# Expert layers of a two-block transformer: where the next expert's tokens are transposed, how weight rows lie on partitions, and when the two down sums run

## The chip, the cores and the metric

One core of one Trainium2 chip runs the whole program in one launch. The metric is the device time in microseconds (us) from launch to end; the kernel before took 3669.67 us as the median of three runs (3669.27 to 3676.42). The core has a matmul engine (PE; its weight loads, PEld, run beside the matmuls), VectorE (DVE), ScalarE (ACT), GpSimd (POOL), SyncE (SP, which here issues loads and stores) and 16 DMA engines.

## The reference

Two blocks over 1024 tokens of width 1024, all float32. The first block has two layers, each a mixer (differential attention, then pooling) with a layer norm, and behind it a mixture of experts with a layer norm. The second block (retention, latent attention, gated linear attention) isn't touched. The change lies in the experts, which run once in each of the two layers of the first block:

```python
# router: one of 4 groups per token, the best 2 of its 8 experts, gates from two softmaxes
xin = xf[tok_pad].reshape(NB, MOE_BLOCK, D)            # tokens sorted by expert, blocks of 128
def run_block(args):
    xb, e = args
    h = jax.nn.silu(xb @ w_gate[e]) * (xb @ w_up[e])   # [128, 1024] @ [1024, 512]
    return h @ w_down[e]                               # [128, 512] @ [512, 1024]
y = lax.map(run_block, (xin, blk_e)).reshape(P, D)
out = jnp.zeros((N, D)).at[tok_pad].add(y * w_pad[:, None])
```

There are 32 experts in a layer; each has 2 MB of gate, 2 MB of up and 2 MB of down weights. 1024 tokens with two experts each make 64 tokens per expert on the average; an expert works in one tile of 128.

## The kernel before, in words

**One expert.** `Moe.run` (L759) goes through the 32 experts of a layer. The tokens of an expert come by an indirect DMA on GpSimd (`gather`, L695) out of `hd` in DRAM into one of four buffers `xg`, one token per partition. `x_t` (L698) transposes them: eight 128 x 128 transposes on PE (L95) into two PSUM tiles `tp` of four blocks each, and a split of each tile (L80, L81) into a high part (ACT, `xgh`) and a low part (DVE, `xgl`), both float32r. In a transpose the tokens are the operand that PE loads, the identity the one that streams. A product in this kernel is three matmuls (`mm3`, L85 to L87): high x high, high x low, low x high.

`gate_up` (L705) takes four pieces of weights of 1 MB each, gate and up for the first 512 rows, then gate and up for the last 512 rows. Each piece is 4 x 3 = 12 matmuls of 512 columns into one of two PSUM sums `gu`; silu (ACT, L720) and a product (DVE, L721) make the hidden values `sgu`. `turn_mid` (L724) transposes these in four blocks (L732) into one tile `tp` and splits it into `hh` and `hl`. `down` (L736) takes two more pieces, the left 512 and the right 512 columns of the down weights, each 12 matmuls into a sum `accy`; ACT scales the sum by the gate (L750), DVE adds the residual from `xg` (L751), and GpSimd scatters the result `yo` to `yd` in DRAM (L752).

**Weights.** SP loads each piece (`load_raw`, L98) into one of nine buffers as they come by turns. Partition p of a piece takes row p of each block of 128 rows: 512 columns, 2 KB, in one run, four of them per partition. ACT and DVE split a piece (`split_w`, L106) into one of four buffers `wcut`, high part first.

**The order of an expert's steps.** The hidden values of expert e-1 are transposed in the middle of the gate and up products of expert e, and its down sums follow these. The text of the loop body at L774 to L785 is, in short:

```python
x = nxt
if e + 1 < 32:
    nxt = self.x_t(buf(e + 1), pool, ps)               # the next expert's tokens
between = lambda: mid.append(self.turn_mid(sg, pool, ps))
nsg = self.gate_up(None, None, x, pool, ps, None if e else nc.gpsimd, between if e else None)
if e > 0:
    down(e - 1, mid[0])
if e + 3 < 32:
    gather(e + 3)
```

The tiles `xgh`, `xgl`, `hh`, `hl`, `yo`, and in PSUM `gu` (two kinds), `accy` and `tp` have two buffers each; the eight PSUM banks are all taken. The token buffer that `gather(e + 3)` fills is the one that `down(e - 1)` has just read.

**What sets the order on the engines.** The text above isn't the order in which an engine works. When the program is built, a planner goes through all instructions with an estimate of the time of each. On every engine it takes the instruction that stands first in the text among those whose operands and buffers are there by its estimate, so an instruction further down may go ahead of one that has to wait in the plan. On the chip each engine then works through its own list strictly in order, and waits by semaphores. SP's list of loads is planned in the same way; a load waits until its buffer has been read.

A rare loop behind the experts (L792 to L810) takes the tokens beyond an expert's 128th with the same helpers and one buffer of weights (`OnePiece`); the trace has no round of it: 64 gathers are all.

Of the kernel before, what the change touches and what calls it, by code (L numbers as in the profile page):

```python
# [27 lines left out]
def host_consts():  # L28
# [12 lines left out]
    # a token's number and its row in the results, less 2048  # L41
# [15 lines left out]
    # rotary frequencies of the second block  # L57
# [12 lines left out]
class Ctx:  # L70
# [18 lines left out]
    def transpose_split(self, src, hi, lo, ps, scale=None):  # L89
        """src [128, 8, 128] f32 -> hi/lo [128, 8, 128-slice] f32r views, transposed by block."""  # L90
        nc = self.nc
        for g in range(2):
            tp = ps.tile([P, 4, P], F32, tag="tp", name=self.name("tp"))
            for k in range(4):
                nc.tensor.transpose(tp[:, k], src[:, 4 * g + k], self.ident)  # L95
            self.split(tp, hi[:, 4 * g:4 * g + 4], lo[:, 4 * g:4 * g + 4])

    def load_raw(self, view, pool, tag):  # L98
        """one piece of weights [128, 2048] as it comes; view: as its columns lie"""
        raw = pool.tile([P, 2048], F32, tag=tag, name=self.name("wraw"))  # L100
        a, b = view.shape[1:]
        raw = raw.rearrange("p (a b) -> p a b", b=b)
        self.nc.sync.dma_start(raw, view)
        return raw

    def split_w(self, raw, pool, tag, lo_eng=None, steps=1):  # L106
        """the same in two float32r parts"""
# [8 lines left out]
    def rsqrt(self, pool, v, shape):  # L116
        """1/sqrt(v) of a few columns"""
        y = pool.tile(shape, F32, tag="rs_y", name=self.name("rs_y"))
        self.nc.gpsimd.tensor_tensor(y, v, self.mhalf[:, 0:shape[1]], op=ALU.pow)  # L119
        return y  # L120


class Weights:
    """buffers of streamed weights: slots (pool, tag) that take the pieces as they come by turns, and one of the split ones"""
# [8 lines left out]
    def load(self, view, slot=None):  # L133
        if slot is None:
            slot = self.slots[self.turn % len(self.slots)]
            self.turn += 1
        return self.g.load_raw(view, *slot)
# [5 lines left out]
class OnePiece:  # L143
    """the same with one buffer of each kind, for loops"""
# [4 lines left out]
    def load(self, view):  # L149
        raw = self.raw.rearrange("p (a b) -> p a b", b=view.shape[2])  # L150
        self.g.nc.sync.dma_start(raw, view)
        return raw
# [7 lines left out]
def phase_qkv(g, x_in, v_sb, fill):  # L160
    """queries and keys of differential attention, transposed, turned and split, to DRAM; values to v_sb"""
# [3 lines left out]
    with tc.tile_pool(name="p1", bufs=1) as p1, tc.tile_pool(name="p1w", bufs=2) as pw, \  # L165
# [4 lines left out]
        for t in range(NT):  # L170
# [4 lines left out]
            g.transpose_split(xn, xh[:, :, t * P:(t + 1) * P], xl[:, :, t * P:(t + 1) * P], ps)  # L175
# [15 lines left out]
                # the halves of the tokens outermost: the first product needs only half of them  # L191
# [42 lines left out]
class Attention:  # L234
    """differential attention of layer 0 up to its normalised heads, transposed: oT"""
# [30 lines left out]
    def spare(self):  # L266
        """a buffer [128, 1024] of the first head's, before its load"""
# [4 lines left out]
    def load(self, h):  # L272
        """queries (both parts on the partitions) and keys (each part twice) of both maps of a head"""
# [14 lines left out]
    def scores(self, h, i):  # L288
        """p0 / s0 - lambda p1 / s1 up to the factor 1 / s0"""
# [66 lines left out]
    def norm(self, h):  # L356
        """rms norm of a head: (o / s0) / sqrt(mean((o / s0) ** 2) + eps)"""
# [22 lines left out]
    def norm_last(self, k):  # L380
        """the same for tiles k and 7 - k of the last head, with its transposes"""
# [32 lines left out]
            # tiles of queries in pairs of a long and a short row of scores; the steps of a pair overlap with those of its neighbours  # L414
# [38 lines left out]
def layer_norm(g, pool, z, dst, gb, eps=1e-5):  # L453
    """dst = (z - mean) / sqrt(var + eps) * gain + bias over the free axis of [128, 1024]"""
# [15 lines left out]
def norm_stats(g, pool, z, eps=1e-5):  # L470
    """scale and shift that normalise the rows of [128, 1024]"""
# [14 lines left out]
def norm_apply(g, z, stats, gb):  # L486
    """the layer norm in place, spread over three engines"""
# [14 lines left out]
class Moe:  # L502
    """mixture of experts of one layer"""

    def __init__(self, g, layer, wp, pool, h, hd, yd):
# [9 lines left out]
        # the pieces of the weights in the order of their use  # L515
        wg, wu, wd = (a[n][layer] for n in ("moe_w_gate", "moe_w_up", "moe_w_down"))
        rows = lambda w, kb: w[kb * 512:kb * 512 + 512].rearrange("(k p) c -> p k c", p=P)
        cols = lambda w, n: w[:, n * 512:n * 512 + 512].rearrange("(k p) c -> p k c", p=P)
        self.views, self.raws = [], []
        for e in range(33):  # L520
            if e < 32:
                self.views += [rows(w[e], kb) for kb in range(2) for w in (wg, wu)]
            if e > 0:
                self.views += [cols(wd[e - 1], n) for n in range(2)]

    def prefetch(self, n):
        # the last pieces leave the middle slots, then the first to the stage that follows
        for _ in range(n):
            left = len(self.views)
            self.raws.append(self.wp.load(self.views.pop(0), self.wp.slots[(6 if left > 3 else 9) - left] if left < 7 else None))  # L530
# [5 lines left out]

    def turn(self, t, ps, pool):
        """one tile of tokens, transposed"""
# [11 lines left out]
    def logits(self, t, hT, ps):  # L550
        """router logits of one tile of tokens"""
# [9 lines left out]
    def temp(self, pool, lead, T, trail, n, dt=F32):  # L561
        """[128, *lead, T, *trail], T up to 4, of one size for all T"""
# [6 lines left out]
    def onehot(self, pool, src, n, tab, tag):  # L569
        """maximum over the last axis and the one-hot of its first place"""  # L570
# [11 lines left out]
    def route(self, t0, t1, pool, ps):  # L582
        """experts, gates and places of the tokens of tiles t0 to t1 - 1; the tables of the first window of slots"""
# [27 lines left out]
        # places: the assignments of the tiles before, and of the tokens before in the same tile  # L611
# [11 lines left out]
        # gates  # L623
# [69 lines left out]
    # one expert  # L693
# [4 lines left out]
    def x_t(self, xg, pool, ps):  # L698
# [3 lines left out]
        g.transpose_split(xg.rearrange("p (k d) -> p k d", d=P), xh, xl, ps)  # L702
        return xh, xl

    def gate_up(self, wg, wu, x, pool, ps, lo_eng=None, between=None):  # L705
        g, nc = self.g, self.g.nc
        acc = [ps.tile([P, 512], F32, tag=f"acc{j}", name=g.name("gu")) for j in range(2)]
        for kb in range(2):
            if kb == 1 and between is not None:
                between()  # L710
            for j, w in enumerate((wg, wu)):
                if w is None:
                    wh, wl = self.next_w(lo_eng)
                else:
                    wh, wl = self.wp.split(self.wp.load(w[kb * 512:kb * 512 + 512].rearrange("(k p) c -> p k c", p=P)))
# [8 lines left out]
    def turn_mid(self, sg, pool, ps):  # L724
        """the hidden values, transposed"""
# [4 lines left out]
        sv = sg.rearrange("p (k d) -> p k d", d=P)  # L730
        for k in range(4):
            nc.tensor.transpose(tp[:, k], sv[:, k], g.ident)  # L732
# [3 lines left out]
    def down(self, wd, mid, xg, gate, yidx, pool, ps, no_dep):  # L736
        """gate[:, 0] * (mid @ wd) + gate[:, 1] * xg to the rows yidx"""
# [3 lines left out]
        for n in range(2):  # L741
            if wd is None:
                wh, wl = self.next_w()
            else:
                wh, wl = self.wp.split(self.wp.load(wd[:, n * 512:n * 512 + 512].rearrange("(k p) c -> p k c", p=P)))
            acc = ps.tile([P, 512], F32, tag="accy", name=g.name("accy"))
            for k in range(4):
# [1283 lines left out]
```

## Time and profile before

| | |
|---|---|
| three runs, median | 3669.67 us (3669.27, 3669.67, 3676.42) |
| span of the profiled execution, first to last instruction | 3678.1 us |
| time of that execution around its span | not listed |
| PE busy in the span | 3337.8 us (91%) |
| DVE / ACT / POOL busy | 2438.9 (66%) / 1825.4 (50%) / 802.7 us (22%) |
| mean granted clock of PE | 0.944 |
| experts of layer 0 | about 715 to 1335 us of the span |
| experts of layer 1 | about 1655 to 2275 us of the span |

Busy shares are averages over stages with different limits, so a stage is read by itself. Times within the trace count from the first instruction. A matmul's duration includes its way through the array, and the next one starts before it ends: the distance between two starts is what one costs (about 0.229 us for 512 columns), not its 0.39 us. L12 is line 12 of the kernel. `tp<-ident,xg` reads: tile `tp` written from `ident` and `xg`.

### The profile page before, as it was taken

How to read it: one execution, taken by the hardware profiler on the slowest of the kernel's cores; microseconds unless marked ns; L12 is line 12 of the kernel's file. 1: busy time of each engine (PE TensorE's matmuls, PEld its weight loads, DVE VectorE, ACT ScalarE, POOL GpSimd, SP SyncE). 2: the span in 40 equal slices, each digit the busy share in tenths (PEclk: the TensorE clock that was granted, in tenths of full speed). 3: DMA queues.
4: the chain of work that ended last, by engine and by line, in shares of the span. 5: the costliest groups of instructions: out<-in, count | busy, mean ns of one | idle time of the engine just before them, and what ended most of it. 6: DMA issues, size and time to landing. Idle time of an engine off the chain costs nothing.

```text
span 3678.1 us, 44264 instructions
## 1 busy us (share of the span) xinstructions
PE 3337.8 (91%) x16820; PEld 2742.3 (75%) x16820; DVE 2438.9 (66%) x2912; ACT 1825.4 (50%) x2509; POOL 802.7 (22%) x591
## 2 busy tenths in 40 slices
PE   8889899799998969979999986699989899998988
PEld 7777777688877758768887765586777688776876
DVE  5564887699988886568998877734256435324753
ACT  3123673388866643317887765212447411234761
POOL 0000441223311123022332211533002223300120
PEclk9999999799999989979999998799999999999999
DMA  6554533499998970238999997311222541123144
GB/s 224 186 205 144 146 81 128 166 369 378 372 363 312 324 250 24 94 138 307 377 371 372 336 318 262 106 36 23 78 103 80 173 133 36 29 72 98 67 132 157
DMA packets 404046, 695.79 MB, mean 189 GB/s; under 512 B 43898, under 2 KB 140956, under 8 KB 403764
## 3 DMA queue, kind: packets, MB, share of 16 engines
q1 hardware_dynamic: 383092, 650.91, 52.5%
q0 software_dynamic: 18432, 33.60, 2.5%
q10 hardware_dynamic: 2304, 8.39, 0.6%
q8 instruction: 135, 2.21, 0.3%
q14 instruction: 83, 0.68, 0.1%
HBM read 625.59 MB, written 98.66 MB: 197 GB/s over the span
## 4 chain that ended last, share of the span: by engine, by line
PE 34%; issue 14%; POOL 6%; DVE 5%; ACT 2%; DMA 2%; POOLq 0%; SPq 0%; ACTq 0%; DVEq 0%
PE A L85 4%; PE A L87 4%; PE A L86 4%; PE acc L87 3%; PE acc L85 3%; PE acc L86 3%; POOL xg L695 3%; PE o L1712 1%; PE T L1691 1%; DMA mx<-mixd 1%; PE S L1659 1%; PE o L1703 1%; POOL rs_y L119 1%; PE S L1660 1%; PE S L1661 1%
## 5 line engine op out<-in xcount | busy, mean ns | idle before, releaser
L81 DVE TENSOR_TENSOR wcut<-wraw,wcut 128x2048 fp32r<-128x2048 f32 (+1 forms) x393 | 878.4, 2263 | 48.6 <-ACT wcut L80 46.2
L80 ACT ACTIVATE wcut<-wraw 128x2048 fp32r<-128x2048 f32 (+1 forms) x401 | 753.1, 1896 | 64.6 <-PE gu L87 43.9
L86 PE MATMUL gu<-wcut,xgh 128*128 128x512 f32 x1024 | 404.9, 395 | 7.3 <-DVE wcut L81 7.3
L85 PE MATMUL gu<-wcut,xgh 128*128 128x512 f32 x1024 | 407.0, 402 | 0.0
L87 PE MATMUL gu<-wcut,xgl 128*128 128x512 f32 x1024 | 402.0, 393 | 0.0
L85 PE MATMUL A<-h,whi 128*128 128x512 f32 (+1 forms) x736 | 288.0, 392 | 6.2 <-ACT h L80 3.3
L87 PE MATMUL A<-h,wlo 128*128 128x512 f32 (+1 forms) x736 | 282.8, 384 | 3.8 <-DVE wlo L81 3.8
L86 PE MATMUL A<-h,whi 128*128 128x512 f32 (+1 forms) x736 | 283.4, 385 | 0.9 <-DVE h L81 0.9
L752 POOL DMA_INDIRECT yd<-yo,idx x64 | 75.7, 1182 | 915.4 <-DVE yo L751 898.2
L695 POOL DMA_INDIRECT xg<-hd,idx x64 | 229.6, 3588 | 44.8 <-DVE idx L685 24.1
L80 ACT ACTIVATE whi<-wraw 128x1024 fp32r<-128x1024 f32 (+2 forms) x86 | 71.1, 856 | 337.2 <-PE A L86 252.9
L86 PEld LDWEIGHTS gu<-wcut,xgh 128*128 128x128 f32 x1024 | 193.1, 189 | 49.8 <-DVE wcut L81 12.2
L87 PEld LDWEIGHTS gu<-wcut,xgl 128*128 128x128 f32 x1024 | 192.5, 188 | 41.0
L85 PEld LDWEIGHTS gu<-wcut,xgh 128*128 128x128 f32 x1024 | 191.8, 188 | 40.0 <-ACT wcut L80 1.6
L86 PE MATMUL accy<-wcut,hh 128*128 128x512 f32 x512 | 213.7, 417 | 0.1
L85 PE MATMUL accy<-wcut,hh 128*128 128x512 f32 x512 | 208.7, 408 | 0.0
L87 PE MATMUL accy<-wcut,hl 128*128 128x512 f32 x512 | 207.9, 406 | 0.2
L81 DVE TENSOR_TENSOR wlo<-wraw,whi 128x1024 fp32r<-128x1024 f32 (+2 forms) x86 | 82.5, 974 | 177.1 <-ACT whi L80 176.9
L85 PEld LDWEIGHTS A<-h,whi 128*128 128x128 f32 x736 | 145.6, 198 | 34.3 <-ACT h L80 4.4
L87 PEld LDWEIGHTS A<-h,wlo 128*128 128x128 f32 x736 | 144.8, 197 | 31.6 <-DVE wlo L81 4.7
L86 PEld LDWEIGHTS A<-h,whi 128*128 128x128 f32 x736 | 145.4, 198 | 27.6 <-issue 3.1
L750 ACT ACTIVATE yo<-accy,sg 128x512 f32<-128x512 f32 x128 | 88.2, 689 | 153.1 <-PE accy L87 152.6
(509 smaller groups left out, 7825.6 us busy)
## 6 DMA issues: line engine op xcount, KB each, us to landing
wraw<-in_moe_w_gate SPq DMA_DIRECT2D x128, 1024.0 KB
wraw<-in_moe_w_up SPq DMA_DIRECT2D x128, 1024.0 KB
wraw<-in_moe_w_down SPq DMA_DIRECT2D x128, 1024.0 KB
spare<-in_ada_w SPq DMA_DIRECT2D x48, 512.0 KB
wraw<-in_w_in SPq DMA_DIRECT2D x40, 512.0 KB
y<-yd SPq DMA_DIRECT2D x16, 1024.0 KB
wraw<-in_attn_w_qkv SPq DMA_DIRECT2D x12, 1024.0 KB
mx<-mixd SPq DMA_DIRECT2D x24, 512.0 KB
```

The lines of the kernel that those rows point to most:

```text
L80: self.nc.scalar.activation(hi, src, AF.Copy)
L81: (lo_eng or self.nc.vector).tensor_tensor(lo, src, hi.bitcast(F32), op=ALU.subtract)
L85: mm(out, wh, xh, start=start, stop=False)
L86: mm(out, wh, xl, start=False, stop=False)
L87: mm(out, wl, xh, start=False, stop=stop)
L119: self.nc.gpsimd.tensor_tensor(y, v, self.mhalf[:, 0:shape[1]], op=ALU.pow)
L695: self.g.nc.gpsimd.indirect_dma_start(out=xg, out_offset=None, in_=self.hd, in_offset=bass.IndirectOffsetOnAxis(ap=idx, axis=0), bounds_ch ...
L750: nc.scalar.activation(y[:, sl], acc, AF.Copy, scale=gate[:, 0])
L752: st = nc.gpsimd.indirect_dma_start(out=self.yd, out_offset=bass.IndirectOffsetOnAxis(ap=yidx, axis=0), in_=y, in_offset=None, bounds_chec ...
L1659: nc.tensor.matmul(s[:, c:c + w], qs[0:96, 0, q], ks[0:96, 0, c:c + w], start=True, stop=False)
L1660: nc.tensor.matmul(s[:, c:c + w], qs[0:96, 0, q], ks[0:96, 1, c:c + w], start=False, stop=False)
L1661: nc.tensor.matmul(s[:, c:c + w], qs[0:96, 1, q], ks[0:96, 0, c:c + w], start=False, stop=not last)
```

## The change

In words:

- **Next tokens.** `x_t(e + 1)` is called inside `gate_up(e)`, between its first and its second half, behind `turn_mid(e - 1)`, and no longer ahead of `gate_up(e)`. For expert 0 there is no `turn_mid` and `x_t(1)` is called alone there.
- **Weight rows in pairs.** Partition p of a block of 256 rows takes rows 2p and 2p + 1. A gate or up piece has still 512 rows, now two runs of 4 KB per partition; a down piece is now 256 full rows of 1024 columns, one run of 8 KB per partition. To match, the transposes of the tokens and of the hidden values read every second column of a block of 256 (`pair_blocks`).
- **Down sums.** A down piece now serves both halves of the columns for half of the rows. Both sums are open over both pieces: piece 0 gives 6 matmuls to each sum, piece 1 the other 6, and then both sums are scaled and added.

The diff, without comments, and without the same edits in the helper classes that pass a width `b` along:

```diff
-    def transpose_split(self, src, hi, lo, ps, scale=None):
+    def transpose_split(self, src, hi, lo, ps):
...
-                nc.tensor.transpose(tp[:, k], src[:, 4 * g + k], self.ident)
+                nc.tensor.transpose(tp[:, k], src[4 * g + k], self.ident)
...
-        raw = raw.rearrange("p (a b) -> p a b", b=b)
-        self.nc.sync.dma_start(raw, view)
-        return raw
+    def load_into(self, raw, view, b=None):
+        by = lambda n: raw.rearrange("p (a b) -> p a b", b=n)
+        self.nc.sync.dma_start(by(view.shape[2]), view)
+        return by(b or view.shape[2])
...
+def even_blocks(x):
+    return [x[:, k] for k in range(KD)]
+def pair_blocks(x):
+    v = x.rearrange("p (a q j) -> p a j q", q=P, j=2)
+    return [v[:, k // 2, k % 2] for k in range(x.shape[1] // P)]
...
+    def rows(w, kb):
+        return w[kb * 512:kb * 512 + 512].rearrange("(a p j) c -> p a (j c)", p=P, j=2), 512
+    def down_rows(w, kb):
+        return w[kb * 256:kb * 256 + 256].rearrange("(a p j) c -> p a (j c)", p=P, j=2), D
...
-        rows = lambda w, kb: w[kb * 512:kb * 512 + 512].rearrange("(k p) c -> p k c", p=P)
-        cols = lambda w, n: w[:, n * 512:n * 512 + 512].rearrange("(k p) c -> p k c", p=P)
...
-                self.views += [rows(w[e], kb) for kb in range(2) for w in (wg, wu)]
+                self.views += [self.rows(w[e], kb) for kb in range(2) for w in (wg, wu)]
...
-                self.views += [cols(wd[e - 1], n) for n in range(2)]
+                self.views += [self.down_rows(wd[e - 1], kb) for kb in range(2)]
...
-        g.transpose_split(xg.rearrange("p (k d) -> p k d", d=P), xh, xl, ps)
+        g.transpose_split(pair_blocks(xg), xh, xl, ps)
...
-        for k in range(4):
-            nc.tensor.transpose(tp[:, k], sv[:, k], g.ident)
+        for k, b in enumerate(pair_blocks(sg)):
+            nc.tensor.transpose(tp[:, k], b, g.ident)
...
-        for n in range(2):
-            if wd is None:
-                wh, wl = self.next_w()
...
-            acc = ps.tile([P, 512], F32, tag="accy", name=g.name("accy"))
-            for k in range(4):
-                g.mm3(acc, hh[:, k], hl[:, k], wh[:, k], wl[:, k], k == 0, k == 3)
-            sl = slice(n * 512, n * 512 + 512)
+        cols = [slice(n * 512, n * 512 + 512) for n in range(2)]
+        accs = [ps.tile([P, 512], F32, tag="accy", name=g.name("accy"), bufs=2) for _ in cols]
+        for kb in range(2):
+            wh, wl = self.next_w() if wd is None else self.one_w(self.down_rows(wd, kb))
+            for acc, sl in zip(accs, cols):
+                for j in range(2):
+                    k = 2 * kb + j
+                    g.mm3(acc, hh[:, k], hl[:, k], wh[:, j, sl], wl[:, j, sl], k == 0, k == 3)
+        for acc, sl in zip(accs, cols):
             nc.scalar.activation(y[:, sl], acc, AF.Copy, scale=gate[:, 0])
             nc.vector.scalar_tensor_tensor(y[:, sl], xg[:, sl], gate[:, 1], y[:, sl], op0=ALU.mult, op1=ALU.add)
...
-                x = nxt
-                if e + 1 < 32:
-                    nxt = self.x_t(buf(e + 1), pool, ps)
-                mid = []
-                between = lambda: mid.append(self.turn_mid(sg, pool, ps))
-                nsg = self.gate_up(None, None, x, pool, ps, None if e else nc.gpsimd, between if e else None)
+                x, mid = nxt, []
+                def between():
+                    nonlocal nxt
+                    if e > 0:
+                        mid.append(self.turn_mid(sg, pool, ps))
+                    if e + 1 < 32:
+                        nxt = self.x_t(buf(e + 1), pool, ps)
+                nsg = self.gate_up(None, None, x, pool, ps, None if e else nc.gpsimd, between)
```

## Rows read from the trace of the kernel before

**Rows 1.** Page, the span in 40 slices: busy tenths of PE and DMA.
```profile
PE   8889899799998969979999986699989899998988
DMA  6554533499998970238999997311222541123144
```

**Rows 2.** Busy time by stretch: length, PE, PEld, DVE, ACT, POOL, clock, DMA share, GB/s.
```profile
800.00:1000.00 200.00, 200.00 (x942) 165.31 (x942) 190.31 (x135) 163.40 (x135) 64.98 (x22) 1.00 1.03 377
1020.00:1290.00 270.00, 245.72 (x1096) 197.65 (x1095) 222.78 (x156) 187.21 (x157) 51.33 (x26) 0.96 0.93 333
1700.00:1940.00 240.00, 240.00 (x1130) 198.35 (x1129) 228.57 (x162) 196.14 (x163) 77.98 (x27) 1.00 1.03 375
1960.00:2230.00 270.00, 246.07 (x1089) 197.67 (x1087) 221.89 (x156) 186.52 (x156) 49.61 (x26) 0.95 0.94 333
```

**Rows 3.** PE's waits, 1000:1300, then 1950:2250: total us, times, longest.
```profile
PE tp L95 <- DMA xg<-hd,idx: 20.5, 6, 4.0
PE gu L86 <- DVE wcut L81: 3.6, 6, 0.6
...
PE tp L95 <- DMA xg<-hd,idx: 20.3, 6, 4.0
PE gu L86 <- DVE wcut L81: 3.7, 6, 0.6
```

**Rows 4.** PE in order of time, layer 0: start, us, instruction, [idle before, releaser].
```profile
806.24 1.03 PE L95 MATMUL tp<-ident,xg 128*128 128x128 f32 x8
...
824.07 1.03 PE L95 MATMUL tp<-ident,xg 128*128 128x128 f32 x8
...
1020.24 1.03 PE L95 MATMUL tp<-ident,xg 128*128 128x128 f32 x8
...
1090.41 0.40 PE L85 MATMUL accy<-wcut,hh 128*128 128x512 f32 x1
1093.93 0.45 PE L95 MATMUL tp<-ident,xg 128*128 128x128 f32 x1 [3.13 <-DMA xg<-hd,idx]
...
1094.60 0.63 PE L87 MATMUL accy<-wcut,hl 128*128 128x512 f32 x1
1095.03 0.63 PE L85 MATMUL accy<-wcut,hh 128*128 128x512 f32 x1
...
1287.05 0.49 PE L95 MATMUL tp<-ident,xg 128*128 128x128 f32 x3
```

**Rows 5.** Scatter, gather and its transposes in order of time; last, all gathers' landing.
```profile
863.03 1.01 POOL L752 DMA_INDIRECT yd<-yo,idx  x1 [11.63 <-DVE yo L751]
...
864.34 4.89 POOL L695 DMA_INDIRECT xg<-hd,idx  x1 [0.30 <-issue]
...
877.57 0.60 PE L95 MATMUL tp<-ident,xg 128*128 128x128 f32 x4
...
DMA to landing us min/median/max: 4.8/10.8/11.6
```

**Rows 6.** The hidden values' transposes and their split, in order of time.
```profile
937.46 0.60 PE L732 MATMUL tp<-ident,sgu 128*128 128x128 f32 x4
...
939.48 0.58 ACT L80 ACTIVATE hh<-tp 128x512 fp32r<-128x512 f32 x1
...
941.81 0.68 DVE L81 TENSOR_TENSOR hl<-tp,hh 128x512 fp32r<-128x512 f32 x1
```

**Rows 7.** DMA queues: packets, MB, share of 16 engines; 840:855, then 1342:1357.
```profile
q1 hardware_dynamic: 2683, 5.33, 96.8%
q0 software_dynamic: 162, 0.45, 7.6%
...
q1 hardware_dynamic: 1524, 5.91, 100.6%
```

**Rows 8.** Groups by line: shapes, count | busy us, mean ns of one | idle before.
```profile
L751 DVE SCALAR_TENSOR_TENSOR yo<-xg,sg,yo 128x512 f32<-128x512 f32 x128 | 95.4, 746 | 46.2 <-ACT yo L750 46.2
...
L95 PEld LDWEIGHTS tp<-ident,xg 128*128 128x128 f32 x512 | 66.0, 148 | 65.3 <-issue 46.6 <-DMA xg<-hd,idx 6.8 <-DVE xgl L81 0.5
```

More of the change, by code (lines that the diff above doesn't have):

```diff
@@ L94, in transpose_split, with load_raw @@
             for k in range(4):
-                nc.tensor.transpose(tp[:, k], src[:, 4 * g + k], self.ident)
+                nc.tensor.transpose(tp[:, k], src[4 * g + k], self.ident)
             self.split(tp, hi[:, 4 * g:4 * g + 4], lo[:, 4 * g:4 * g + 4])
-    def load_raw(self, view, pool, tag):
-        raw = pool.tile([P, 2048], F32, tag=tag, name=self.name("wraw"))
-        a, b = view.shape[1:]
-        raw = raw.rearrange("p (a b) -> p a b", b=b)
-        self.nc.sync.dma_start(raw, view)
-        return raw
+    def load_raw(self, view, pool, tag, b=None):
+        return self.load_into(pool.tile([P, 2048], F32, tag=tag, name=self.name("wraw")), view, b)
+    def load_into(self, raw, view, b=None):
+        by = lambda n: raw.rearrange("p (a b) -> p a b", b=n)
+        self.nc.sync.dma_start(by(view.shape[2]), view)
+        return by(b or view.shape[2])
     def split_w(self, raw, pool, tag, lo_eng=None, steps=1):
@@ L131, in use, with load @@
         self.slots, self.turn = slots, turn
-    def load(self, view, slot=None):
+    def load(self, view, slot=None, b=None):
         if slot is None:
@@ L136, in load @@
             self.turn += 1
-        return self.g.load_raw(view, *slot)
+        return self.g.load_raw(view, *slot, b)
     def split(self, raw, lo_eng=None):
@@ L147, in __init__, with load @@
         self.g, self.raw, self.cut = g, raw, cut
[L149 to L152, printed above, removed]
+    def load(self, view, slot=None, b=None):
+        return self.g.load_into(self.raw, view, b)
     def split(self, raw):
@@ L174, in phase_qkv @@
             nc.sync.dma_start(xn, x_in[t * P:(t + 1) * P, :].rearrange("p (k d) -> p k d", d=P))
-            g.transpose_split(xn, xh[:, :, t * P:(t + 1) * P], xl[:, :, t * P:(t + 1) * P], ps)
+            g.transpose_split(even_blocks(xn), xh[:, :, t * P:(t + 1) * P], xl[:, :, t * P:(t + 1) * P], ps)
         rope = p1.tile([64, 2, S], F32, name="rope")
@@ L502 @@
 class Moe:
+    @staticmethod
+    def rows(w, kb):
+        return w[kb * 512:kb * 512 + 512].rearrange("(a p j) c -> p a (j c)", p=P, j=2), 512
+    @staticmethod
+    def down_rows(w, kb):
+        return w[kb * 256:kb * 256 + 256].rearrange("(a p j) c -> p a (j c)", p=P, j=2), D
     def __init__(self, g, layer, wp, pool, h, hd, yd):
@@ L529, in prefetch @@
             left = len(self.views)
-            self.raws.append(self.wp.load(self.views.pop(0), self.wp.slots[(6 if left > 3 else 9) - left] if left < 7 else None))
+            view, b = self.views.pop(0)
+            self.raws.append(self.wp.load(view, self.wp.slots[(6 if left > 3 else 9) - left] if left < 7 else None, b))
     def next_w(self, lo_eng=None):
@@ L535, in next_w, with one_w @@
         return self.wp.split(self.raws.pop(0), lo_eng)
+    def one_w(self, piece):
+        view, b = piece
+        return self.wp.split(self.wp.load(view, b=b))
     def turn(self, t, ps, pool):
@@ L714, in gate_up @@
                 else:
-                    wh, wl = self.wp.split(self.wp.load(w[kb * 512:kb * 512 + 512].rearrange("(k p) c -> p k c", p=P)))
+                    wh, wl = self.one_w(self.rows(w, kb))
                 for k in range(4):
@@ L729, in turn_mid @@
         tp = ps.tile([P, 4, P], F32, tag="tp", name=g.name("tp"))
-        sv = sg.rearrange("p (k d) -> p k d", d=P)
-        for k in range(4):
-            nc.tensor.transpose(tp[:, k], sv[:, k], g.ident)
+        for k, b in enumerate(pair_blocks(sg)):
+            nc.tensor.transpose(tp[:, k], b, g.ident)
         g.split(tp, hh, hl)
@@ L740, in down @@
         y = pool.tile([P, D], F32, tag="yo", name=g.name("yo"))
-        for n in range(2):
-            if wd is None:
-                wh, wl = self.next_w()
-            else:
-                wh, wl = self.wp.split(self.wp.load(wd[:, n * 512:n * 512 + 512].rearrange("(k p) c -> p k c", p=P)))
-            acc = ps.tile([P, 512], F32, tag="accy", name=g.name("accy"))
-            for k in range(4):
-                g.mm3(acc, hh[:, k], hl[:, k], wh[:, k], wl[:, k], k == 0, k == 3)
-            sl = slice(n * 512, n * 512 + 512)
+        cols = [slice(n * 512, n * 512 + 512) for n in range(2)]
[7 more added lines that the diff above has]
+        for acc, sl in zip(accs, cols):
             nc.scalar.activation(y[:, sl], acc, AF.Copy, scale=gate[:, 0])
@@ L1942, in program @@
                         sl = slice(t % 4 * P, t % 4 * P + P)
-                        g.transpose_split(z.rearrange("p (k d) -> p k d", d=P), *(x[:, :, sl] for x in x2[t // 4]), tps)
+                        g.transpose_split(even_blocks(z.rearrange("p (k d) -> p k d", d=P)), *(x[:, :, sl] for x in x2[t // 4]), tps)
                 W = []
```

## The prediction

> **What bounds the kernel now.** I read the page first. The two expert layers are the parts of the sliced row in which the matmul engine (PE) and the DMA engines stand at 9 together [rows 1]; counted from 0, slices 8 to 14 and 18 to 24 of 40, 7 x 92 us each. The change touches nothing else that costs time, so the question is what ends last there. The view by stretches splits each layer in two [rows 2]. Among the earlier experts (800 to 1000 us, 1700 to 1940 us) PE is busy all the time at clock 1.00: the rate is PE's own, with VectorE (DVE) at 95% and the DMA share at 1.03, both close behind. From expert 19 on (1020 to 1290, 1960 to 2230) PE is busy 245.7 of 270 us, its clock is 0.96 and 0.95, and all other engines do less. No engine became slower there; something waits.
>
> The view of waits names it: in each layer six waits of the transposes of an expert's tokens for their gather, 20.5 and 20.3 us, and six short ones for a low part of weights, 3.6 and 3.7 us [rows 3]. The stretch before 1000 us has none. The order of time shows where [rows 4]. In the steady part the eight transposes stand behind the last product of a down sum, one expert every 824.07 - 806.24 = 17.83 us. In the late part they stand inside the down sum: one product of it (1090.41), then a transpose that waits 3.13 us, then products 0.43 us apart (1094.60, 1095.03) instead of 0.23: the clock fell from 2.4 to 1.2 GHz while PE stood. So the planned order moved the transposes ahead of products whose weights it thought late. On the chip those weights were there: no PE wait for weights longer than 0.6 us is in the view.
>
> Why the gather is then late: its buffer is free when the result of expert e-1 has left, and it fills expert e+3's. In the steady part the scatter goes at 863.03, the gather at 864.34 and takes 4.89 us on GpSimd; the median from issue to landing is 10.8 us [rows 5], so about 875.1, and PE takes the tokens at 877.57. That is 2.4 us to spare. Transposes pulled one down sum ahead (24 products of 0.229 us, 5.5 us) miss it by 3.1 us, which is the wait seen.
>
> **The change, part by part.** The stretch's loss, from rows: waits 20.5 + 3.6 + 20.3 + 3.7 = 48.1 us [rows 3]; half clock (1 - 0.96) x 270 + (1 - 0.95) x 270 = 24.3 us [rows 2]; together 72.4. As a check: from the transposes of expert 18 (1020.24) to those of expert 31 (1287.05) are 266.8 us [rows 4], against 13 x 17.83 = 231.8; 35.0 lost, where layer 0's share of the sum is 20.5 + 3.6 + 10.8 = 34.9.
>
> Transposes of the next tokens in the middle of gate and up: the same eight per expert, now behind 24 products and the four transposes of the hidden values. The gather gains 24 x 0.229 + 0.36 = 5.9 us, to 8.3 us of slack in the planned order. The work is the same on PE, ACT and DVE; the split tokens are wanted only after 24 gate and up products and the 24 of the down sum, so their splits hide. Gain: all 72.4 us if the transposes stay where the text has them. At each layer's start expert 1's transposes leave the path to the first product: 0 to 2 us, taken as 0.
>
> What is late next is their buffer. The hidden values take one PSUM buffer, the tokens two, out of the same two; before, 5.5 us of products lay between, now nothing. The second four must wait until the hidden values are split. In the trace those transposes start at 937.46, ACT copies at 939.48, and DVE, behind three weight splits, subtracts from 941.81 for 0.68 us [rows 6]: 5.0 us after their start. Behind PE's wait would be queued all products of the second half. The order hides it if some 18 of these 24 products (18 x 0.229 = 4.1 us) go first. Bounds: 0, or 4.2 us for each of 62 experts, 260 us, with nothing between. I take 0: the planned order has shown that it fills a wait with ready products.
>
> Rows in pairs: the transposes read every second element. They are the loaded (stationary) operand: eight take 1.03 us, 0.11 us apart, a load lasts 148 ns in the mean [rows 4, 8]. No row shows such a read with a step. Bounds: 0, as the same 128 columns go in, or double, 0.11 x 12 x 64 = 84 us. I take 0, the rows' own price. The Trainium skill (SBUF — State Buffer, Specifications (TRN2)) says that memory gives its full rate when at least two accesses fall in each 16-byte line; a step of 8 bytes just does. By that rule the sum stays, without it the 84 us would come; no run here shows it.
>
> Weights: 2 KB packets become 4 KB (gate, up) and 8 KB (down). With 2 KB packets 5.33 MB took 96.8% of 16 engines for 15 us, 43.6 engine-us per MB; loads in 4 KB rows took 100.6% for 5.91 MB, 40.9 [rows 7]. An expert's 6.29 MB: 274 / 16 = 17.1 us before, 257 / 16 = 16.1 after; gathers and scatters add 7.6% of the time, 1.4 us. DMA goes from 18.5 us, over PE's 17.83, to 17.5, under it. Alone it gains 0: nine buffers of weights lie between, and PE never waited long for them. It is cover for the case that everything runs at 17.83.
>
> Both down sums open: the same 24 products. The first half's result (VectorE's part is 0.75 us, [rows 8]) is no longer taken beside the second half's products but just before the second's. The second leaves as before, so scatter and gather move by 0 to 0.75 us, against 8.3 us of slack; 0. The next down sum comes 12 us later, so the two accumulators are free in time. VectorE's order changes, not its 17 us per expert (0.95 x 17.83, [rows 2]).
>
> Sum: 72.4 us. The page's span is 3678.1 us; the time around that execution isn't listed, but the span alone is 8.4 us over the median of 3669.67, so I subtract from the median and take differences of spans as differences of times: 3669.67 - 72.4 = **3597 us**.
>
> **Rivals.**
> (a) The order doesn't do what the text says. In the plan the transposes of expert e+1 are ready as soon as gate and up of e-1 are done, in the old text and the new; what pulled them ahead was a plan that saw weights late from expert 19 on, in both layers alike. If its estimate of the loads doesn't shrink with longer packets, they are pulled to the same place and wait as now. For it: a shift of 52 places may be no bar where 24 was none. Against: the hidden values' transposes now come first, and loads may count as shorter. Time: 3670, less up to 1 us for each of 12 waits, as transfers are 6% shorter, and a few half-clock spells: 3645 to 3672, 3662 in the middle.
> (b) The plan sees weights late only for the last experts: half the loss stays, 3634.
> (c) Slower: PE stands at the second four transposes for their buffer. Place: middle of gate and up, each expert. It decides from the point where fewer than 18 products stand ahead. With 12, 1.4 us x 62 = 87: 3684; with 6, 2.8 us x 62 = 174, and half clock after the longer waits: over 3771. Below 1.2 us per expert the change still gains.
> (d) Slower: stepped reads double the transposes: 3597 + 84 = 3681.
>
> **How the numbers follow.** About 0.2%, 7 us, is what a measurement of this kernel can tell. Forecast 0.42 (its own range 3588 to 3612); (a) 0.26, of it 0.12 faster, 0.10 same, 0.04 slower; (b) 0.08; (c) 0.14, of it 0.02 same, 0.12 slower; (d) 0.10, of it 0.03 same, 0.07 slower. Faster 0.42 + 0.12 + 0.08 = 0.62, same 0.15, slower 0.23. The range runs from a little under the forecast, 3586, to 3690: it takes in (a), (b), (d) and the mild half of (c); some 0.12 lie outside.
>
> **What would show it.** Right: the layers' late stretches have PE at 100% and clock 1.00 with 17.83 us per expert to the end; no wait for a gather behind expert 0; the DMA share falls below 1.0; token transposes lie in two fours with products between, in the middle of gate and up; an eight's spacing stays 0.11 us. Wrong: waits of about 3 us for a gather from expert 19 on (a); waits of token transposes for VectorE's low part of the hidden values (c); transposes 0.2 us apart (d).

## The result and the profile after

| | before | after |
|---|---|---|
| median of the runs, us | 3672.07 | 3633.61 |
| range, us | 3669.27 to 3676.42 | 3625.14 to 3635.93 |
| span of the profiled execution, us | 3678.1 | 3630.7 (time 3632.52) |
| mean granted clock of PE | 0.944 | 0.952 |

The ratio is 0.9892, 95% interval 0.9879 to 0.9904: 38.5 us faster, 1.1%. The forecast was 3597 us, in a range of 3586 to 3690: the sign and the wide range hold, but 34 of the 72 us did not come, and the time lies outside the 3588 to 3612 us that the forecast's own case was given. The views below go in the order of the rows of before.

The page of the changed kernel, the span in 40 slices, against [rows 1]:

```profile
PE   8889899799999969979999995799989899998988
DMA  6554623499999960248999996211222542122245
```

The experts still hold both engines at 8 and 9, in the same slices; the last one of the second layer (24) falls from 6 to 5 on PE and from 7 to 6 on DMA. The view by stretches, same four as [rows 2] (length, PE, PEld, DVE, ACT, POOL, clock, DMA share, GB/s):

```profile
800.00:1000.00 200.00, 200.00 (x939) 166.94 (x938) 190.56 (x135) 163.07 (x135) 74.79 (x22) 1.00 1.00 384
1020.00:1290.00 270.00, 263.53 (x1201) 211.53 (x1199) 244.43 (x172) 202.54 (x172) 52.60 (x27) 1.00 0.93 349
1700.00:1940.00 240.00, 240.00 (x1125) 200.24 (x1124) 227.78 (x163) 193.58 (x161) 85.81 (x26) 1.00 1.00 382
1960.00:2230.00 270.00, 259.85 (x1173) 206.96 (x1171) 243.98 (x175) 199.62 (x169) 51.71 (x28) 1.00 0.92 336
```

The early stretches are full as before, the DMA share fell from 1.03 to 1.00. The late ones rose from 245.7 and 246.1 to 263.5 and 259.9 us of PE, at clock 1.00 where it was 0.96 and 0.95. They are not full; the second reaches some 3 us past the layer's last product. PE's waits, 1000:1300 and then 1950:2250, against [rows 3]:

```profile
PE gu L86 <- DVE wcut L81: 7.0, 25, 0.7
...
PE gu L86 <- DVE wcut L81: 6.9, 25, 0.7
PE accy L87 <- DVE hl L81: 0.6, 1, 0.6
```

All twelve waits for a gather are gone, 40.8 us. The waits for low parts of weights went from 6 to 25 per layer. PE in order of time, first early experts, then late ones, against [rows 4]:

```profile
865.74 0.63 PE L754 MATMUL tp<-ident,sgu 128*128 128x128 f32 x4
866.20 0.64 PE L95 MATMUL tp<-ident,xg 128*128 128x128 f32 x4
866.60 0.47 PE L85 MATMUL gu<-wcut,xgh 128*128 128x512 f32 x1
...
867.14 0.39 PE L87 MATMUL gu<-wcut,xgl 128*128 128x512 f32 x1
...
871.04 0.63 PE L95 MATMUL tp<-ident,xg 128*128 128x128 f32 x4
...
884.13 0.64 PE L95 MATMUL tp<-ident,xg 128*128 128x128 f32 x4
...
1134.46 0.64 PE L95 MATMUL tp<-ident,xg 128*128 128x128 f32 x4
...
1140.68 0.63 PE L95 MATMUL tp<-ident,xg 128*128 128x128 f32 x4
...
1159.66 0.63 PE L95 MATMUL tp<-ident,xg 128*128 128x128 f32 x4
1160.04 0.71 PE L85 MATMUL gu<-wcut,xgh 128*128 128x512 f32 x2
1161.08 0.50 PE L86 MATMUL gu<-wcut,xgh 128*128 128x512 f32 x1 [0.33 <-DVE wcut L81]
...
1176.04 0.50 PE L86 MATMUL gu<-wcut,xgh 128*128 128x512 f32 x1 [0.18 <-DVE wcut L81]
```

Early: the two fours of tokens lie 4.84 us apart with 19 products between them and no wait; one expert takes 884.13 - 866.20 = 17.93 us, where before it took 17.83. Late: 1159.66 - 1140.68 = 18.98 us. Two products take 1.04 us there (1160.04 to 1161.08) that take 0.54 behind the same transposes early (866.60 to 867.14); the view of waits shows 0.33 us of that. A second wait, of 0.18 us, follows in each late expert (1176.04). The late period begins at expert 19 in both layers, as before, and there the plan still pulls transposes ahead: the first four of an expert's tokens lie ahead of gate and up (1134.46), only the second four in its middle (1140.68).

GpSimd around an early scatter and gather, and all gathers' landing, against [rows 5]:

```profile
863.64 5.01 POOL L774 DMA_INDIRECT yd<-yo,idx  x1 [10.50 <-DVE yo L773]
868.95 2.12 POOL L718 DMA_INDIRECT xg<-hd,idx  x1 [0.30 <-issue]
...
1121.26 2.70 POOL L718 DMA_INDIRECT xg<-hd,idx  x1 [0.30 <-issue]
...
DMA to landing us min/median/max: 4.2/9.5/12.3
```

868.95 + 9.5 is 878.5; the tokens are wanted at 884.13, so 5.7 us of slack, forecast 8.3: the scatter ahead of it now takes 5.01 us, not 1.01. Late there is less: the gather issued at 1121.26 landed 11.0 us later, and its tokens' first four start at 1134.46, 2.2 us after. For the tokens of experts 20 to 31 this slack is 1.0 to 3.5 us in the two layers. The hidden values' transposes and split, against [rows 6], are as they were:

```profile
937.42 0.63 PE L754 MATMUL tp<-ident,sgu 128*128 128x128 f32 x4
...
939.45 0.58 ACT L80 ACTIVATE hh<-tp 128x512 fp32r<-128x512 f32 x1
...
941.78 0.69 DVE L81 TENSOR_TENSOR hl<-tp,hh 128x512 fp32r<-128x512 f32 x1
```

The DMA queue of the loads in 840:855, against [rows 7], and two groups by line, against [rows 8]:

```profile
q1 hardware_dynamic: 1198, 5.61, 97.8%
...
L773 DVE SCALAR_TENSOR_TENSOR yo<-xg,sg,yo 128x512 f32<-128x512 f32 x128 | 93.2, 748 | 9.0 <-ACT yo L772 8.7
...
L95 PEld LDWEIGHTS tp<-ident,xg 128*128 128x128 f32 x512 | 77.1, 205 | 12.4 <-DMA xg<-hd,idx 6.7
```

97.8% of 16 engines for 15 us is 234.7 engine-us for 5.61 MB, 41.8 per MB (before 43.6, forecast 40.9). The load of a token transpose went from 148 to 205 ns.

What ends the late waits is seen on ACT and DVE, in order of time:

```profile
1164.42 3.71 ACT L80 ACTIVATE wcut<-wraw 128x2048 fp32r<-128x2048 f32 x2
1171.17 0.69 ACT L772 ACTIVATE yo<-accy,sg 128x512 f32<-128x512 f32 x1 [3.04 <-PE accy L87]
1171.76 1.91 ACT L80 ACTIVATE wcut<-wraw 128x2048 fp32r<-128x2048 f32 x1
...
1173.70 2.29 DVE L81 TENSOR_TENSOR wcut<-wraw,wcut 128x2048 fp32r<-128x2048 f32 x1 [1.05 <-ACT wcut L80]
```

In the early order ACT splits three pieces behind `sgu` before it takes both halves of `yo`. In the late order it takes the first half of `yo` behind two pieces, waits 3.04 us for it, and only then splits the third. That piece's low part stands on DVE behind the high part (1.05 us), and PE's next piece of gate and up stands behind that low part (the 0.18 us at 1176.04). From there DVE has no pause, and the piece after it comes late too (the 0.3 us waits, as at 1161.08).

**Theory** from these rows: the place of the transposes brought the gain; what is missing lies in the planned order of the late experts, where ACT stands in `yo`, and the two open sums make it worse, since with them `yo` is ready behind the 18th of 24 products and not behind the 12th. **Rivals:** the longer packets brought the gain; weights are really late in the late part.

### The profile page after: what moved, and what is told of

Same layout as the page of the kernel before. It is cut to its first block, busy times and chain, and to the rows that moved or that the text cites. A ratio compares the mean times of both kernels' runs of the same rounds, so it can differ in the third digit from the quotient of the medians.

```text
span 3630.7 us, 44256 instructions
## 1 busy us (share of the span) xinstructions
PE 3325.3 (92%) x16820; PEld 2733.2 (75%) x16820; DVE 2443.4 (67%) x2912; ACT 1818.7 (50%) x2509; POOL 821.1 (23%) x591
## 4 chain that ended last, share of the span: by engine, by line
PE 46%; DVE 7%; ACT 3%; issue 3%; POOL 3%; DMA 2%; SPq 0%; POOLq 0%; ACTq 0%; DVEq 0%
PE A L87 4%; PE A L85 4%; PE A L86 4%; PE acc L87 3%; PE acc L85 3%; PE acc L86 3%; PE gu L86 3%; PE gu L87 2%; PE gu L85 2%; DVE wcut L81 2%; PE accy L85 1%; PE accy L87 1%; PE accy L86 1%; PE T L1717 1%; PE o L1738 1%
## 5 line engine op out<-in xcount | busy, mean ns | idle before, releaser
L774 POOL DMA_INDIRECT yd<-yo,idx x64 | 187.2, 2925 | 857.5 <-DVE yo L773 836.2
L86 PE MATMUL accy<-wcut,hh 128*128 128x512 f32 x512 | 203.1, 397 | 0.0
L87 PE MATMUL accy<-wcut,hl 128*128 128x512 f32 x512 | 200.6, 392 | 1.1 <-DVE hl L81 1.1
L85 PE MATMUL accy<-wcut,hh 128*128 128x512 f32 x512 | 191.7, 393 | 0.0
L718 POOL DMA_INDIRECT xg<-hd,idx x64 | 136.4, 2131 | 44.9 <-DVE idx L708 24.1
```

Source lines behind the costliest of these rows:

```text
L85: mm(out, wh, xh, start=start, stop=False)
L86: mm(out, wh, xl, start=False, stop=False)
L87: mm(out, wl, xh, start=False, stop=stop)
L718: self.g.nc.gpsimd.indirect_dma_start(out=xg, out_offset=None, in_=self.hd, in_offset=bass.IndirectOffsetOnAxis(ap=idx, axis=0), bounds_ch ...
L774: st = nc.gpsimd.indirect_dma_start(out=self.yd, out_offset=bass.IndirectOffsetOnAxis(ap=yidx, axis=0), in_=y, in_offset=None, bounds_chec ...
```

## Experiments

Each was timed in five rounds against the kernel before, whose median beside them was 3671.4 to 3672.5 us.

**The move alone** (before with `x_t(e + 1)` in the middle; rows and down sums as they were).

```diff
-                x = nxt
-                if e + 1 < 32:
-                    nxt = self.x_t(buf(e + 1), pool, ps)
-                mid = []
-                between = lambda: mid.append(self.turn_mid(sg, pool, ps))
...
+                x, mid = nxt, []
+                def between():
+                    nonlocal nxt
+                    if e > 0:
+                        mid.append(self.turn_mid(sg, pool, ps))
+                    if e + 1 < 32:
+                        nxt = self.x_t(buf(e + 1), pool, ps)
...
```

> The kernel before with one edit: the next tokens are transposed between the halves of gate and up. Weights come in 2 KB rows and the down sums follow one another as before. Theory (the order of the transposes gave the gain, the transfers did not): no wait for a gather behind expert 0 and clock 1.00 to the end of both layers; transposes at 0.11 us, period 17.83 us in the early experts; a late part with waits for weight parts as in the changed kernel; time 3615 to 3645 us. Rival (the longer packets gave the gain): the move alone brings little, 3655 to 3675 us, and PE waits for weights that DMA brings late.

Measured 3610.97 us, ratio 0.9834 (0.9822 to 0.9847): faster than the whole change. Its late stretch, and the second four of a late expert's tokens and of the next but one's:

```profile
1020.00:1290.00 270.00, 266.34 (x1245) 216.59 (x1243) 251.84 (x177) 214.02 (x177) 40.86 (x28) 1.00 1.01 364
...
1171.59 0.60 PE L95 MATMUL tp<-ident,xg 128*128 128x128 f32 x4
...
1208.18 0.60 PE L95 MATMUL tp<-ident,xg 128*128 128x128 f32 x4
```

Two late experts take 36.59 us, 18.3 each in the mean. The gain is the move's, and the other two parts together cost 23 us in this order.

**Everything but the move** (`x_t(e + 1)` back ahead of gate and up).

> The changed kernel with the next tokens' transposes back in the text ahead of gate and up; pairs of rows and both down sums stay. Theory (order): the transposes of late experts are pulled into the down sum again and wait about 3 us each for the gather, from about expert 19 on in both layers; 3655 to 3690 us, no faster than the kernel before. Rival (packets gave the gain): no such waits or shorter ones, 3630 to 3645 us.

Measured 3651.46 us, ratio 0.9942 (0.9933 to 0.9951). Neither: it lies between the two. Its waits in 1000:1290:

```profile
PE gu L86 <- DVE wcut L81: 6.4, 25, 0.3
PE tp L95 <- DMA xg<-hd,idx: 4.3, 7, 1.4
```

The gather waits are back, but 1.4 us at most in this layer (2.0 in the other) and not 4.0, and the granted clock of the stretch is 1.00, not 0.96. The order there is another (three transposes behind the 14th product of the down sum), and its late experts, at 18.4 to 22.4 us, may leave the gather more time; that is argued and not tested. I had not thought of it; without the move 20 us of the 72 can be had, and which of the other two parts brings them is open.

**Single rows** (no pairs: 2 KB rows for gate and up, full rows of 4 KB for down, no step).

```diff
-  w[kb * 512:kb * 512 + 512].rearrange("(a p j) c -> p a (j c)", p=P, j=2)
+  w[kb * 512:kb * 512 + 512].rearrange("(a p) c -> p a c", p=P)
...
```

> The changed kernel without pairs: gate and up in single rows (2 KB per packet), down in single full rows (4 KB), transposes without a step; the move and both open down sums stay. Theory (order; the step costs 0.1 us per expert; the transfers are only cover): the same order, DMA share above 1.00 in the early experts, 3622 to 3636 us. Rival (packets gave part of the gain): PE waits for weights in the layers, 3645 us or more.

Measured 3630.47 us, ratio 0.9884 (0.9870 to 0.9899), with the DMA share at 1.02 in the early experts (800 to 1000 us). Its PE takes the experts' work in the same order as the changed kernel, instruction by instruction, and so do ACT and DVE: the plan doesn't see the length of packets. In this order longer packets are worth nothing that can be measured; the cleanest pair is this kernel and the next, which differ in the weight rows alone and have no step (3630.47 and 3627.41 us, overlapping intervals). Against the move alone, timed beside it, this kernel differs by the open down sums and the full down rows that these need: 19.5 us slower.

**No step** (`pair_blocks` takes neighbouring columns).

> The changed kernel with the transposes of tokens and hidden values reading 128 neighbouring columns instead of every second of 256; the weights still come in pairs, so columns and weight rows no longer belong together and the output isn't the reference's. Theory (the step costs 0.09 us per expert): period 17.83 instead of 17.92 us, loads of the transposes 140 instead of 207 ns, 3626 to 3630 us. Rival (the longer loads are hidden and the longer period has another cause): period 17.92 us, 3632 to 3636 us.

Measured 3627.41 us, ratio 0.9885 (0.9871 to 0.9900); the interval overlaps the changed kernel's, so the time alone decides nothing. The trace does: early experts take 17.83 us, and the load is

```profile
L95 PEld LDWEIGHTS tp<-ident,xg 128*128 128x128 f32 x512 | 62.8, 143 | 17.0 <-DMA xg<-hd,idx 6.6
```

143 ns against 205. The step costs 62 ns a load, of which PE shows 0.09 us per expert, 64 x 0.09 = 6 us.

**Down sums apart** (the changed kernel with the down sums of before).

```diff
-        accs = [ps.tile([P, 512], F32, tag="accy", ...) for _ in cols]
+        for n in range(2):
+            acc = ps.tile([P, 512], F32, tag="accy", ...)   # one sum, one piece of 512 columns
...
```

> The changed kernel with the down sums one after the other again, each over one piece of 512 columns (2 KB rows, hidden values transposed without a step); the move and the pairs of gate and up rows stay. Theory (the two open sums cost the late part 20 us, because yo is ready only behind the 18th of 24 products): late periods of 18.75 and 17.9 us in turn as with the move alone, 3611 to 3619 us (8 of 12 transposes keep the step). Rival (the pairs cost it): 3627 us or more.

Measured 3614.20 us, ratio 0.9835 (0.9817 to 0.9854): as the theory has it. Undoing this part of the change, with the full down rows and the step of the hidden values that belong to it, gains 19 us. Its late PE time is that of the move alone (266.28 of 270 us).

**The order held** (the changed kernel; each step of an expert chained to the last instruction of the step before, on PE, ACT and DVE, in the order of the early experts).

```diff
+    @contextmanager
+    def step(self):
+        with ExitStack() as st:
+            for ins in list(self.last.values()):       # the last one on PE, ACT, DVE
+                st.enter_context(self.tc.issue_after(ins.ins))
+            yield
...
```

> The changed kernel with the order of its early experts held for experts 1 to 31: edges that set only the order of issue chain the steps on PE, ACT and DVE, so that the result yo is scaled behind three weight splits and the down sum isn't broken. Work, loads and buffers are the same. Theory (the late part's 19.0 us come from the planned order, in which ACT stands about 3 us in yo ahead of weights that are there): period 17.92 us to the end, no wait of PE for a low part, 24 x 1.1 = 26 us less than the changed kernel, 3602 to 3614 us. Rival (weights really come late in the late part, the plan is right): PE waits for weights in the held order too, 3625 us or more.

Measured 3613.79 us, ratio 0.9833 (0.9815 to 0.9851), at the upper end of what was expected. Its late stretches:

```profile
1020.00:1290.00 270.00, 270.00 (x1255) 222.62 (x1254) 256.18 (x180) 218.27 (x179) 76.88 (x28) 1.00 0.98 365
1960.00:2190.00 230.00, 230.00 (x1069) 189.49 (x1068) 218.24 (x157) 186.18 (x152) 64.80 (x25) 1.00 0.96 362
```

PE is full to the end: with pairs, weights are not late. But every expert takes 18.05 us, not 17.92.

**The order held on PE alone** (edges for PE only).

> As the changed kernel with the order held, but with the edges on PE alone; ACT and DVE follow the plan, in which late experts scale yo with a weight split between its halves. Theory (ACT's place of yo is the cause): part of the late loss stays, with waits of PE for low parts, 3612 to 3628 us. Rival (PE's own broken down sum is the cause): all of it goes, 3602 to 3611 us.

Measured 3653.26 us, ratio 0.9943 (0.9927 to 0.9959), slower than either theory had it. PE's order is that of the kernel above (but for the order within six neighbouring products at 32 places in late down sums), and only ACT's and DVE's are planned, yet 39 us lie between them. The profiled execution took 3643.43 us, 10 us less than the median. Its waits of PE in 1000:1290, and ACT late:

```profile
PE gu L95 <- DVE wcut L81: 9.1, 12, 0.8
PE accy L95 <- DVE wcut L81: 2.8, 12, 0.2
...
1167.84 3.71 ACT L80 ACTIVATE wcut<-wraw 128x2048 fp32r<-128x2048 f32 x2
1173.59 0.69 ACT L819 ACTIVATE yo<-accy,sg 128x512 f32<-128x512 f32 x1 [2.03 <-PE accy L96]
1174.18 1.90 ACT L80 ACTIVATE wcut<-wraw 128x2048 fp32r<-128x2048 f32 x1
```

The same picture: `yo` behind two pieces, a wait, the third piece late, PE behind its low part. So ACT's and DVE's order is enough to make the late part slow while PE's down sum is whole; what PE's broken down sum costs by itself no run shows. A period of 19.49 us came out; that it would be worse than in the free order I had not expected.

**The move alone, order held.**

> The kernel with the move alone (2 KB rows, down sums one after the other, no step), with the order of its early experts held for experts 1 to 31. Theory: 17.83 us per expert to the end of both layers, so what is left of the late loss, 24 experts by 0.48 us, goes: 3595 to 3604 us. Rival (2 KB rows need 18.5 us of DMA per expert, more than PE's 17.83, and the late part is then bound by DMA): no gain, 3606 us or more.

Measured 3609.50 us, ratio 0.9828 (0.9810 to 0.9846): no gain over the move alone. The time is in the rival's range, but PE was nearly full: each expert took 17.97 us instead of 17.83, which hid what the next one shows.

**21 products between the two fours, order held**: the move alone, and then the changed kernel.

```diff
-            gu(acc[1], w1, 1, (0, 1))
+            gu(acc[1], w1, 1, (0, 1, 2))      # then the second four, then the rest
...
```

> The kernel with the move alone and the order held, with 21 products instead of 18 between the two fours of token transposes. Theory (in the held order the second four stand 0.14 us per expert at their PSUM buffer, because 18 products are a little too few): 17.83 instead of 17.97 us, 62 x 0.14 = 9 us less than 3609.5: 3598 to 3604 us. Rival (the edges themselves cost the 0.14 us): no gain, 3607 us or more.

> The changed kernel with the order held, with 21 products instead of 18 between the two fours of token transposes. Theory as above: 17.92 instead of 18.05 us per expert, 62 x 0.13 = 8 us less than 3613.8: 3603 to 3609 us. Rival: no gain, 3611 us or more.

Measured 3613.60 us, ratio 0.9837 (0.9823 to 0.9850), and 3600.59 us, ratio 0.9806 (0.9792 to 0.9819): the first in its rival's range, though not for its reason, the second better than its theory. Both now run at their own rate, 17.83 and 17.91 us, under the same edges, so 18 products were too few: in the changed kernel the way from the last product ahead of the second four to the second of these transposes took 0.48 us with 18 and 0.34 us with 21. That stands in starts alone; it is too short for the view of waits. The first kernel keeps 17.83 us only up to expert 24 in the first layer and 22 in the second. Late, with what ACT waits for in 1130:1240:

```profile
1150.97 0.60 PE L775 MATMUL tp<-ident,xg 128*128 128x128 f32 x4
...
1169.42 0.60 PE L775 MATMUL tp<-ident,xg 128*128 128x128 f32 x4
...
ACT wcut L80 <- DMA wraw<-in_moe_w_down: 7.6, 10, 0.8
ACT wcut L80 <- DMA wraw<-in_moe_w_gate: 4.3, 6, 0.8
ACT wcut L80 <- DMA wraw<-in_moe_w_up: 4.0, 10, 0.9
```

18.45 us per expert, ACT behind DMA: with 2 KB rows the loads are the bound once the nine buffers' lead is used up. The second, with pairs:

```profile
1175.29 0.63 PE L797 MATMUL tp<-ident,xg 128*128 128x128 f32 x4
...
1187.44 0.63 PE L763 MATMUL tp<-ident,sgu 128*128 128x128 f32 x4
1187.91 0.64 PE L797 MATMUL tp<-ident,xg 128*128 128x128 f32 x4
...
1193.20 0.63 PE L797 MATMUL tp<-ident,xg 128*128 128x128 f32 x4
```

1193.20 - 1175.29 = 17.91 us to the end, no wait of ACT for DMA in that stretch. Between these two kernels the pairs and the open sums gain 13 us, where in the planned order they cost 23. This is the fastest kernel of the study.

**The kernel before, order held.** The first of two kernels held another order than the expectation says: it put the tokens of expert e + 1 right ahead of their own products, one expert later than the kernel before has them.

> The kernel before, with nothing of the change, but with the order of its own early experts held for experts 1 to 31 (next tokens behind the down sum, ahead of gate and up, on PE; the matching order on ACT and DVE). Theory (the loss before lay in the planned order, not in the place of the transposes in the text): no gather wait behind expert 0, clock 1.00 to the end of the layers, 17.83 to 18.0 us per expert, 3597 to 3610 us. Rival (without the move the gather, with 2.4 us to spare, or DMA with 2 KB rows becomes late over a layer): waits for gathers or weights, 3625 us or more.

Measured 3756.15 us, ratio 1.0227 (1.0213 to 1.0241). It says only what tokens without a lead cost: PE waits 0.4 us for their high part and 1.5 us for their low part, 20.26 us for most experts. The second has the order of before:

> The kernel before, nothing of the change, with the order of its early experts held for experts 1 to 31 as that kernel has it: the tokens of expert e + 1 behind the down sum of e - 2, a whole gate and up ahead of their products (the earlier kernel with this aim had them one expert later). Theory (the order alone lost the time; the move is not needed for the gather): no gather wait behind expert 0, 17.83 us per expert until 2 KB rows make weights late from about expert 23 on, then 18.45 us: 3603 to 3618 us. Rival (2.4 us of slack are not enough for the gather over a whole layer): PE waits for gathers, 3625 us or more.

Measured 3621.19 us, ratio 0.9860 (0.9838 to 0.9881), 3 us over what was expected. 17.83 us per expert up to expert 26 in the first layer and 22 in the second; then weights come late, and with them, here in 1000:1290,

```profile
PE tp L775 <- DMA xg<-hd,idx: 3.2, 2, 1.7
```

the gather. Some 13 us of the time are a fault of this kernel's start (in each layer the way from the third expert's tokens to the fourth's takes 24.69 and 24.30 us instead of 17.82, as ACT splits weights ahead of the first hidden values). So the order alone, with nothing of the change, brings 51 us. Without the move the gather has too little slack only where something else is late.

## Why the prediction was right, and where it was not

The direction and the main mechanism were right. That the time lies in the range says little for the sum, since the range was stretched to take in the rivals. Of the signs named for being right, the end of the gather waits and the clock of 1.00 came, and in the early experts the two fours in the middle of gate and up; PE at 100% with 17.83 us to the end did not (263.5 and 259.9 of 270 us, 18.98 us), and the DMA share fell to 1.00 and not below.

- **What bounded the kernel**, a planned order that takes transposes ahead of their gather: right. Holding that kernel's own early order gained 51 us with no other edit.
- **The move**, 72.4 us from 40.8 + 7.3 us of waits and 24.3 us of half clock: the gather waits and the half clock went, as forecast, though not with the slack forecast: 8.3 us were worked out for transposes that stay where the text has them, and late the plan pulled the first four ahead and left 1.0 to 3.5 us. Alone the move gained 60 us, since the late order came back to 18.3 and not to 17.83 us.
- **Both down sums at 0**: this is the step that failed. I asked when accumulators and buffers are free and how much VectorE has to do, and not when `yo` becomes ready against the weight splits that stand behind it on ACT. It cost 19 us (sums apart) to 19.5 us (single rows against the move alone). That VectorE has 17 us of work either way was true and beside the point: an engine that works strictly in order loses by what stands at its head.
- **The sum**: it took the late part back to the early rate. The late rate was 18.98 us: 12 experts x 1.06 x 2 layers is 25 us. Whole layers, from the first token transpose to the last down product, take 591.9 and 591.4 us against 575.9 and 576.0 with the order held and 21 products, 31 us in all. With the step's 6 us either sum accounts for about the 34 us between 72.4 and 38.5.
- **The step at 0**: 64 x 0.09 = 6 us, between the ends given (0 and 84). The Trainium skill (SBUF — State Buffer, Specifications (TRN2)), by whose rule a step of 8 bytes keeps the full rate, is not borne out by this row: the load took 205 ns against 143. PE hides most of that, so neither reading gave the price.
- **Weights**: 18.5 us of DMA per expert with 2 KB rows was right where it could be seen, 18.45. With pairs I had 17.5; 41.8 engine-us per MB give 16.4 + 1.4 = 17.8. "Alone it gains 0, cover for the case that everything runs at 17.83" held: nothing in the planned order, and needed in the held one.
- **Rivals.** (a) is half right: the plan's order doesn't change with the packets' length (single rows), and it did pull transposes ahead from expert 19 on; but they come after the gather has landed, by 1.0 us at the least, and no wait follows. (b) has the number, 3634, and the words "sees weights late only for the last experts", but not the mechanism: the order changes at expert 19 as before, and what was late on the chip was ACT's third split. (c): no wait in the planned order with 19 products between; with 18 it began, 0.13 us per expert, so the point from which it decides was placed rightly. (d) is out.

What stays open: why the order with PE alone held is worse (19.49 us) than the free one, and what PE's own late order costs where ACT and DVE are held; no such kernel was run.

## What to carry to other kernels

Where a planner orders the work, ask of each edit what it does to the place of every result on an in-order engine: one that becomes ready later, at the same place in the list, holds up all that is ready behind it. Compare the rate of an undisturbed stretch with that of a disturbed one, and don't count the whole difference as gain before it is plain what order the disturbed one will get. A relief on a second resource, here longer packets, can be worth nothing until the first bound is gone; then it decides.

## What was unexpected of the hardware

- An indirect DMA's time on GpSimd moved between its two kinds: the scatter from 1.01 to 5.01 us, the gather from 4.89 to 2.12, at the same sizes, in the early experts of the two kernels. What set it was not tested.
- A stationary operand read with a step of 8 bytes took 205 ns instead of 143 to load, 1.4 times and not double.
- 25 waits of 7.0 us in a view stood for 12 x 1.06 = 13 us of loss per layer: a product's row lasts 0.39 us and the next starts after 0.229, so a pause shows as idle only beyond the end of the row, and a short wait costs more than its row says (1.04 us for two products instead of 0.54, row 0.33).
